# RWKV output products grouped with the heads in turn, tokens of block two's second half made early, and the adaptive vectors moved beside the first feed-forward half

## The chip, the cores and the metric

One core of a Trainium2 chip runs the whole program; the other cores are idle. The metric is the device time of one execution in microseconds (us). All values are 32-bit floats in memory. A large matrix product is done as three products of a split operand (high and low part, "fp32r"): `lo*high`, `high*lo`, `high*high`, all added up in PSUM. The small products (RWKV, attention, gated linear attention) are plain float32, and TensorE executes each of them as two passes, so 128 float32 products in the source are 256 matmul rows in the profile.

## The reference, cut to what matters

Two blocks follow each other on 1024 tokens of width 1024. Block one: RMS norm, one input projection, sliding-window attention with 8 heads (2 key heads), an RWKV-7 recurrence with 8 heads of 64, an output projection, and a convolution-gated feed-forward part of width 4096. Block two: an RMS norm that is scaled and shifted by "adaptive" vectors, an input projection, two gated linear attentions, a stick-breaking attention, an output projection and a final norm.

```python
# RWKV, per head and token (block one)
sa = einsum('bhvk,bhk->bhv', state, -kk_t)
state = state * w_t + sa[..., None] * (kk_t * a_t) + v_t[..., None] * k_t
o_t = einsum('bhvk,bhk->bhv', state, r_t)
# attention scores (block one)
scores = einsum('bnqhgd,bnkhd->bnhgqk', q, kb) * HEAD_DIM ** -0.5 + bias
# adaptive vectors and the tokens of block two
ada = silu(c) @ w_ada + b_ada                  # (1, 1024) @ (1024, 3072)
shift, scale, gate = split(ada, 3)
h = rms_norm_2(x) * (1.0 + scale) + shift
p = h @ w_in                                   # block two's projection
```

## The kernel before, in words

The program is recorded by generators ("streams") that `weave` steps in turn, each by a clock of its own: a `yield 5.2` moves the stream 5.2 units ahead, and the stream that stands earliest is stepped next. A scheduler then fixes the order on each engine from what was recorded, with priorities (`tc.high_priority(offset=...)` lets a part go ahead of what was recorded before it). Each engine runs its list in order. All loads and stores go through one queue, SyncE's (SP), also in order. Three stages follow each other.

**Stage one** (to about 592 us): the projection of block one (`proj1`, products `g`, L151), attention (`attention`, score products L664 into `a_ps`), RWKV for the first half of the tokens in three streams `rwkv_a`, `rwkv_b`, `rwkv_c`, and the output projection of the first half (`out_rows`).

**Stage two** (592 to about 1930 us): the feed-forward part, one half of the tokens after the other (`ffn`: products `g` with `w_up`, products `d` with `w_down`). Beside the first half runs RWKV for the second half of the tokens (`rest`). `between` waits until that is done, then makes the output projection of the second half, norms it for the second feed-forward half, computes the adaptive vectors (`ada_vectors`), and later begins block two's projection for the first half.

**Stage three** (from about 1930 us): block two. `fill` issues block two's remaining projection units of the first half (`units(0, ORD[0])`, 18 of them), then `proj2(1)`, which norms, scales, shifts and transposes the four 128-token tiles of the second half (`pre2`, `to_h`), then the units of the second half and the output projection. Beside it run the gated attentions (`gla_a`, `gla_b`, `gla_c`) and the stick-breaking attention (`stick`).

`rwkv_c` works on 128 tokens (a chunk pair, `e` = 0 to 7) in two steps `c` of 64 tokens. Heads lie in pairs: head `h` of a pair stands in partitions 64h to 64h+63, and the four pairs are counted by `j`. Per step there are four groups of eight products: with the state `St` for the solve (L594), the state update (`ra<-UV,BKt`, L601), and the output in two parts that add up in PSUM, `AR*St` (L606, contraction over one head's 64 rows) and `MT*UV` (L608, contraction over 128 rows). `ou[0]` and `ou[1]` are the PSUM tiles of the two heads. L606 and L608 alternate, product by product.

`ada_vectors` loads `w_ada` in 24 pieces of 512 KB (`wa`, two buffers), multiplies each with a column of `c` and adds it up on VectorE (`adam`, L81), sums over the partitions with a product by ones (L950), adds the bias and stores the vector.

Helper lines: L75 is every ScalarE activation, L78 tensor-tensor, L81 scalar-tensor-tensor and L85 tensor-scalar on VectorE, L125 the power on GpSimd, L135 the load of a weight piece (`wr`), which ScalarE and VectorE split into `wh` and `wl`; three such buffers are in use in turn.

## Time and profile before

| | |
|---|---|
| time, median of 3 runs | 2600.23 us (2585.8 to 2609.15) |
| the profiled execution | 2600.69 us |
| its span, first to last instruction | 2598.9 us |
| mean granted TensorE clock in it | 0.968 |
| TensorE (PE) busy | 2480.5 us, 95% |
| VectorE (DVE) busy | 1695.4 us, 65% |
| ScalarE (ACT) busy | 1171.0 us, 45% |

The profile shows this one execution. "PE" is the time in which a matmul is under way, "PEld" the loading of its stationary operand, which overlaps. A row `g<-hi,wl` reads: written `g`, read `hi` and `wl`. A line number is one of the kernel before. The granted clock is the share of TensorE's full clock that its throttle lets through. A row of the timeline gives the start in us, the time from the first start to the last end in us, engine, line, operation, tiles, shapes, the number of instructions in a row (x), and the idle time ahead of it with what ended it. In the order of a program, a row stands for one product (or xN for N equal ones in a row), and has no time.

### The profile page before, as it was taken

How to read it: one execution, taken by the hardware profiler on the slowest of the kernel's cores; microseconds unless marked ns; L12 is line 12 of the kernel's file. 1: busy time of each engine (PE TensorE's matmuls, PEld its weight loads, DVE VectorE, ACT ScalarE, POOL GpSimd, SP SyncE). 2: the span in 40 equal slices, each digit the busy share in tenths (PEclk: the TensorE clock that was granted, in tenths of full speed). 3: DMA queues.
4: the chain of work that ended last, by engine and by line, in shares of the span. 5: the costliest groups of instructions: out<-in, count | busy, mean ns of one | idle time of the engine just before them, and what ended most of it. 6: DMA issues, size and time to landing. Idle time of an engine off the chain costs nothing.

```text
span 2598.9 us, 40965 instructions
## 1 busy us (share of the span) xinstructions
PE 2480.5 (95%) x15310; PEld 1940.4 (75%) x15310; DVE 1695.4 (65%) x3676; ACT 1171.0 (45%) x2205; POOL 99.4 (4%) x138
## 2 busy tenths in 40 slices
PE   7999999899999999999988999999999989999987
PEld 5777777678787787878776888778887766777665
DVE  5466653664675674755687655545567897878887
ACT  4344332463433533334443333443345665566864
POOL 1001000000000000000000000000000000000000
PEclk9999998889999999999999999999999989999988
DMA  6433223542232332324486432243346425342437
GB/s 205 145 111 102 69 77 100 159 128 81 86 97 72 94 94 69 96 70 130 136 278 199 130 98 94 83 130 121 94 139 208 132 97 159 123 129 77 143 132 251
DMA packets 219998, 320.78 MB, mean 123 GB/s; under 512 B 56956, under 2 KB 95508, under 8 KB 219799
## 3 DMA queue, kind: packets, MB, share of 16 engines
q1 hardware_dynamic: 219798, 318.17, 38.9%
q8 instruction: 120, 1.97, 0.3%
q14 instruction: 80, 0.65, 0.1%
HBM read 270.88 MB, written 47.21 MB: 122 GB/s over the span
## 4 chain that ended last, share of the span: by engine, by line
PE 73%; DVE 10%; issue 6%; DMA 4%; ACT 4%; POOL 2%; SPq 0%; POOLq 0%; DVEq 0%; ACTq 0%
PE g L151 37%; PE d L151 11%; PE gr L743 2%; DVE wl L78 1%; PE gr L744 1%; PE gr L745 1%; DMA wa<-in_w_ada_dram 1%; PE ou L608 1%; PE ou L606 1%; PE R L1463 1%; PE ra L495 1%; PE s L1359 1%; PE a_ps L698 1%; DMA wr<-in_w_out_dram 1%; PE x L743 1%
## 5 line engine op out<-in xcount | busy, mean ns | idle before, releaser
L75 ACT ACTIVATE wh<-wr 128x512 fp32r<-128x512 f32 x712 | 443.7, 626 | 664.3 <-PE g L151 223.2
L151 PE MATMUL g<-hi,wl 128*128 128x512 f32 (+1 forms) x1680 | 678.0, 404 | 7.9 <-DVE wl L78 3.4
L151 PE MATMUL g<-hi,wh 128*128 128x512 f32 (+1 forms) x1680 | 668.9, 398 | 0.0
L151 PE MATMUL g<-lo,wh 128*128 128x512 f32 (+1 forms) x1680 | 667.6, 397 | 0.0
L78 DVE TENSOR_TENSOR wl<-wr,wh 128x512 fp32r<-128x512 f32 x712 | 484.4, 684 | 224.9 <-ACT wh L75 223.1
L151 PEld LDWEIGHTS g<-hi,wl 128*128 128x128 f32 (+1 forms) x1680 | 317.6, 189 | 86.3 <-issue 6.3
L151 PEld LDWEIGHTS g<-hi,wh 128*128 128x128 f32 (+1 forms) x1680 | 317.5, 189 | 72.5 <-issue 3.1
L151 PEld LDWEIGHTS g<-lo,wh 128*128 128x128 f32 (+1 forms) x1680 | 317.8, 189 | 71.6 <-issue 5.1
L81 DVE SCALAR_TENSOR_TENSOR cv<-g,CW,cv 128x511 f32<-128x511 f32 (+1 forms) x256 | 190.5, 744 | 186.0 <-ACT cv L75 185.8
L151 PE MATMUL d<-hh,wl 128*128 128x512 f32 x512 | 204.1, 403 | 7.1 <-DVE wl L78 2.2
L151 PE MATMUL d<-hl,wh 128*128 128x512 f32 x512 | 202.8, 396 | 0.1
L151 PE MATMUL d<-hh,wh 128*128 128x512 f32 x512 | 201.9, 395 | 0.0
L75 ACT ACTIVATE cv<-g,CW 128x512 f32<-128x512 f32 x128 | 99.5, 777 | 195.3 <-PE g L151 195.1
L78 DVE TENSOR_TENSOR acc<-d,acc 128x512 f32<-128x512 f32 x112 | 76.5, 688 | 83.4 <-PE d L151 83.3
L151 PEld LDWEIGHTS d<-hh,wl 128*128 128x128 f32 x512 | 96.9, 190 | 34.3 <-DVE acc L78 4.4
L151 PEld LDWEIGHTS d<-hl,wh 128*128 128x128 f32 x512 | 97.2, 190 | 22.5 <-DVE hl L78 2.8
L151 PEld LDWEIGHTS d<-hh,wh 128*128 128x128 f32 x512 | 97.1, 190 | 20.2
L743 PE MATMUL gr<-wl,hi 128*128 128x512 f32 x200 | 84.7, 424 | 6.3 <-DVE wl L78 4.6
L744 PE MATMUL gr<-wh,lo 128*128 128x512 f32 x200 | 81.0, 405 | 1.7 <-DVE lo L78 1.7
L745 PE MATMUL gr<-wh,hi 128*128 128x512 f32 x200 | 80.4, 402 | 0.0
L125 POOL TENSOR_TENSOR rs<-ms,half_c 128x1 f32<-128x1 f32 x48 | 31.1, 650 | 1129.4 <-DVE ms L85 1118.7
L75 ACT ACTIVATE hh<-cv 128x512 fp32r<-128x512 f32 x64 | 40.4, 631 | 70.1 <-DVE cv L78 69.7
(484 smaller groups left out, 3634.0 us busy)
## 6 DMA issues: line engine op xcount, KB each, us to landing
wr<-in_w_up_dram SPq DMA_DIRECT2D x256, 256.0 KB, 2.7
wr<-in_w_in_dram SPq DMA_DIRECT2D x160, 256.0 KB, 2.8
wr<-in_w_down_dram SPq DMA_DIRECT2D x128, 256.0 KB, 2.7
wr<-in_w_out_dram SPq DMA_DIRECT2D x100, 256.0 KB, 2.9
wr<-in_w_values_dram SPq DMA_DIRECT2D x64, 256.0 KB, 2.8
xt<-x SPq DMA_DIRECT2D x24, 512.0 KB, 4.6
wa<-in_w_ada_dram SPq DMA_DIRECT2D x24, 512.0 KB, 4.7
xt<-in_x_dram SPq DMA_DIRECT2D x16, 512.0 KB, 3.7
```

What stands on the lines that cost most here:

```text
L75: S.activation(out=out, in_=in_, func=func, **kw)
L78: (eng or V).tensor_tensor(out=out, in0=in0, in1=in1, op=op)
L81: V.scalar_tensor_tensor(out=out, in0=in0, scalar=scalar, in1=in1, op0=op0, op1=op1)
L125: G.tensor_tensor(out=dst, in0=src, in1=half_c[0:src.shape[0], 0:src.shape[1]], op=ALU.pow)
L151: T.matmul(out=ps, lhsT=l, rhs=r, start=(first and n == 0), stop=(last and n == 3 * len(wk) - 1))
L495: T.matmul(out=gp[:, q, :], lhsT=flat(BK[hb:hb + 64, 4 * b + q, :, :]), rhs=flat(AR[hb:hb + 64, 4 * b + q, 0:2, :]), start=True, stop=True)
L606: T.matmul(out=ou[h][ob:ob + 64, 0, j, :], lhsT=AR[hb:hb + 64, 2 * j + c, 0, :], rhs=St[hb:hb + 64, j, :], start=True, stop=False)
L608: T.matmul(out=ou[h][ob:ob + 64, 0, j, :], lhsT=MT[:, 2 * j + c, h, 0:64], rhs=UV[:, 2 * j + c, hb:hb + 64], start=False, stop=True)
L698: T.matmul(out=pv[:, h, :], lhsT=pt[:, i, kb, :], rhs=vtok[:, n - 1 + kb, 64 * g:64 * g + 64], start=(kb == kbs[0]), stop=(kb == 1))
L743: T.matmul(out=p, lhsT=hi[:, k, tok], rhs=wl, start=first, stop=False)
L744: T.matmul(out=p, lhsT=lo[:, k, tok], rhs=wh, start=False, stop=False)
L745: T.matmul(out=p, lhsT=hi[:, k, tok], rhs=wh, start=False, stop=last)
```

## The change

- In `rwkv_c`, the products with the state (L594) go with the heads in turn instead of one head after the other; the eight products `AR*St` of the output (L606) are issued together, ahead of the state update, and the eight products `MT*UV` (L608) together behind it. Only the first product into each PSUM tile and step has the start flag.
- In `attention`, the score products of the two key heads, which lie in partitions 0 to 63 and 64 to 127, go in turn: two PSUM tiles are taken together, and four products fill them by turns.
- `ada_vectors` runs at the start of `between`, so beside the first feed-forward half and the RWKV of the second half, with 14 units of its clock behind each load; its sum over partitions uses `psd`, the PSUM tiles of `w_down`'s products.
- `proj2(1)` is split: `prepare2` norms, scales and shifts the four tiles of block two's second half behind the eleventh unit of `units(0, ...)`, two of them in `xs` buffers and two in place in `xt` buffers; `proj2(1)` then only transposes them, at a priority of 250 ahead. `rstd_halves` is code that stood in `pre1` and is now called from both places.

Lines of the changed kernel are numbered a little higher: L594, L601, L606, L608 and L664 became L601, L616, L610, L621 and L676; L135, L151, L78, L81 and L85 became L137, L153, L80, L83 and L87.

```diff
+NP2, AP2 = 11, 250
+YA = 14
...
         for c in range(2):
             ob = 64 * c
+            for j in range(4):
+                for h in range(2):
+                    hb = 64 * h
+                    T.matmul(out=ou[h][0:64, 1, j, :], lhsT=AR[hb:hb + 64, 2 * j + c, 1, :], rhs=St[hb:hb + 64, j, :],
+                             start=True, stop=True)
             for h in range(2):
                 hb = 64 * h
-                for j in range(4):
-                    T.matmul(out=ou[h][0:64, 1, j, :], lhsT=AR[hb:hb + 64, 2 * j + c, 1, :], rhs=St[hb:hb + 64, j, :],
-                             start=True, stop=True)
                 tt(UV[0:64, c:8:2, hb:hb + 64], ou[h][0:64, 1], UV[0:64, c:8:2, hb:hb + 64], ADD)
+
+            for j in range(4):
+                for h in range(2):
+                    hb = 64 * h
+                    T.matmul(out=ou[h][ob:ob + 64, 0, j, :], lhsT=AR[hb:hb + 64, 2 * j + c, 0, :], rhs=St[hb:hb + 64, j, :],
+                             start=j == 0, stop=True, skip_group_check=True)
             sp = psr_t([128, 4, 64])
...
             for j in range(4):
                 for h in range(2):
                     hb = 64 * h
-                    T.matmul(out=ou[h][ob:ob + 64, 0, j, :], lhsT=AR[hb:hb + 64, 2 * j + c, 0, :], rhs=St[hb:hb + 64, j, :],
-                             start=True, stop=False)
                     T.matmul(out=ou[h][ob:ob + 64, 0, j, :], lhsT=MT[:, 2 * j + c, h, 0:64], rhs=UV[:, 2 * j + c, hb:hb + 64],
-                             start=False, stop=True)
+                             start=False, stop=True, skip_group_check=True)
...
-            for w in range(4):
-                g = w % 2
-                sp = psa_t([128, 2, 256])
...
+            for w in (0, 2):
+                sps = [psa_t([128, 2, 256]) for _ in range(2)]
                 for i in range(2):
...
+                    for g in range(2):
+                        T.matmul(out=sps[g][:, i, ko:], lhsT=qt[64 * g:64 * g + 64, w + i, :],
+                                 rhs=kT[64 * g:64 * g + 64, k0:k0 + nk], start=True, stop=True)
...
+        def total(w, m):
+            bb = ap.tile([128, D], F32, name="wa", bufs=2)
+            SY.dma_start(out=bb, in_=a["b_ada"][:, w * D:(w + 1) * D].broadcast_to([128, D]))
+            yield YA
+            for b in range(2):
+                ps = psd_t([128, 512])
...
-                yield 1.5
...
+                yield YA
+            yield from total(w, m)
...
     def between():
 
         nonlocal ap, shp, ps_x, evp
+        pa = ExitStack()
+        ap = pool("ap", 1, stack=pa)
+        yield from ada_vectors()
+        pa.close()
         yield from after(("c", 7))
...
         py.close()
-        pa = ExitStack()
-        ap = pool("ap", 1, stack=pa)
-        yield from ada_vectors()
-        pa.close()
+        yield 0.1
         yield from after(("g", 1, G1))
...
+    def prepare2():
+
+        yield from need1_x2()
+        scale1, shift = pre2_weights()
+        for i in range(4):
+            if i < 2:
+                xs = new_xs()
+                pre2(4 + i, xs, scale1, shift)
+            else:
+                xs = xt_load(x2_d[4 + i])
+                r = rstd_halves(xs)
+                stt(xs, xs, r, scale1, MUL, MUL)
+                tt(xs, xs, shift, ADD)
+            ready.append(xs)
+            yield 1.5
...
             hi, lo = new_h()
-            w = pre2_weights()
             for i in range(4):
-                xs = new_xs()
-                pre2(4 + i, xs, *w)
-                to_h(xs, i, hi, lo)
-                yield 3
+                with tc.high_priority(offset=AP2):
+                    to_h(ready.pop(0), i, hi, lo)
+                yield 1
...
     def fill():
-        yield from units(0, ORD[0], psg_t)
+        yield from units(0, ORD[0][:NP2], psg_t)
+        yield from prepare2()
+        yield from units(0, ORD[0][NP2:], psg_t)
         yield from proj2(1)
```

Three places show how the instructions move. The first is TensorE in stage one, the output products of the first 128 tokens (`ou_1858` and `ou_1859` are the two heads' PSUM tiles; `ra` is the state update, `g` the projection). Before:

```order
L601 MATMUL ra<-UV,BKt 64x64 x7
L606 MATMUL ou_1859<-St,AR 64x64
L608 MATMUL ou_1859<-UV,MT 64x64
L608 MATMUL ou_1858<-UV,MT 64x64
L606 MATMUL ou_1859<-St,AR 64x64
L608 MATMUL ou_1859<-UV,MT 64x64
L606 MATMUL ou_1858<-St,AR 64x64
L608 MATMUL ou_1858<-UV,MT 64x64
L606 MATMUL ou_1859<-St,AR 64x64
L608 MATMUL ou_1859<-UV,MT 64x64
```

The same place in the changed program (`ou_1864` and `ou_1865` are the two heads), and behind it the second step:

```order
L610 MATMUL ou_1864<-St,AR 64x64 x4
L610 MATMUL ou_1865<-St,AR 64x64 x4
L616 MATMUL ra<-UV,BKt 64x64 x8
L621 MATMUL ou_1864<-UV,MT 64x64
L621 MATMUL ou_1865<-UV,MT 64x64
L621 MATMUL ou_1864<-UV,MT 64x64
L621 MATMUL ou_1865<-UV,MT 64x64
```

```order
L610 MATMUL ou_1864<-St,AR 64x64 x4
L621 MATMUL ou_1864<-UV,MT 64x64 x4
L700 MATMUL a_ps<-C,st 128x128 x2
L610 MATMUL ou_1865<-St,AR 64x64 x4
L621 MATMUL ou_1865<-UV,MT 64x64 x4
```

The alternation of two kinds of product is gone: a kind now comes in runs of four or eight. Of the 128 products of L610 over all 16 steps, 88 stand in 22 runs of four, 32 in 4 runs of eight, and 8 in runs of one and seven; of those of L621, 72 stand in 18 runs of four, 48 in 6 runs of eight, and 8 in runs of three and five. The products of L610 go one head after the other, not in turn; those of L601, with the state, go in turn everywhere.

The second place is the queue of SyncE at the start of the first feed-forward half (`CW` are the convolution's weights, `wr` a piece of `w_up` or `w_down`, `mixk` and `xt` rows of activations, `wa` a piece of `w_ada`). Before:

```order
L845 DMA CW<-in_params_dram 128x256
L737 DMA mixk<-mix_d_133 128x512 x2
L135 DMA wr<-in_w_up_dram 128x512 x10
L135 DMA wr<-in_w_down_dram 128x512 x6
L463 DMA AR<-rkv_d_2_131 128x2x64 x3
```

In the changed program:

```order
L859 DMA CW<-in_params_dram 128x256
L968 DMA wa<-in_w_ada_dram 128x1024 x2
L236 DMA xt<-in_x_dram 128x1024
L137 DMA wr<-in_w_up_dram 128x512
L968 DMA wa<-in_w_ada_dram 128x1024 x2
L137 DMA wr<-in_w_up_dram 128x512
L968 DMA wa<-in_w_ada_dram 128x1024
L137 DMA wr<-in_w_up_dram 128x512
L968 DMA wa<-in_w_ada_dram 128x1024
L137 DMA wr<-in_w_up_dram 128x512 x2
L968 DMA wa<-in_w_ada_dram 128x1024 x2
L137 DMA wr<-in_w_up_dram 128x512 x2
```

The eight loads of the first vector stand one for one among the first `w_up` pieces of the half. The loads of the second and the third vector stand further behind, each again by turns with one `wr` piece.

The third place is VectorE in stage three, where the tokens of block two's second half are made (`xs` or `xt` is a tile of 128 tokens, `rs` its norm factor, `gbc` the scale, `shift` the shift; `PT`, `se`, `mk`, `XL` belong to the attentions). Before, the first two tiles are made early, and the last two stand among the stick-breaking attention's work, right ahead of their transposes:

```order
L81 SCALAR_TENSOR_TENSOR xs<-xt,rs,gbc 128x1024
L1367 TENSOR_REDUCE PT<-mk 128x64
L78 TENSOR_TENSOR xs<-xs,shift 128x1024
L81 SCALAR_TENSOR_TENSOR se<-w,se 128x2x128
L85 TENSOR_SCALAR ms<-ss 128x1
L1395 TENSOR_REDUCE ssn<-tmp 128x8
L78 TENSOR_TENSOR se<-se,C_16659 128x2x128
L81 SCALAR_TENSOR_TENSOR xs<-xt,rs,gbc 128x1024
```

In the changed program the last two tiles stand right behind the first two, some 260 rows earlier:

```order
L80 TENSOR_TENSOR xt<-xt,shift 128x1024
L80 TENSOR_TENSOR wl<-wr,wh 128x512
L80 TENSOR_TENSOR ms<-ss_17752 128x1
L80 TENSOR_TENSOR wl<-wr,wh 128x512
L87 TENSOR_SCALAR ms<-ms 128x1
L83 SCALAR_TENSOR_TENSOR xt<-xt,rs,gbc 128x1024
L80 TENSOR_TENSOR xt<-xt,shift 128x1024
```

On TensorE the stretch without any projection product `g` ahead of `proj2(1)` goes from 219 products to 131, counted product by product.

More of the change, by code (lines that the diff above doesn't have):

```diff
@@ L313, in pre1 @@
                 xs = xt
[L314 to L322 removed]
+                r = rstd_halves(xt)
             stt(xs, xt, r, gbc, MUL, MUL)
```

59 lines of the change are left out of this document (30 added, 29 removed).

## The prediction

> **What bounds the kernel now.** I read the busy times first, then the chain of work that ended last, then windows that cut the span into stages.
>
> ```profile
> PE 2480.5 (95%) x15310; PEld 1940.4 (75%) x15310; DVE 1695.4 (65%) x3676; ACT 1171.0 (45%) x2205; POOL 99.4 (4%) x138
> PE 73%; DVE 10%; issue 6%; DMA 4%; ACT 4%; POOL 2%; SPq 0%; POOLq 0%; DVEq 0%; ACTq 0%
> ```
>
> TensorE (PE) is busy 95% of the span and holds 73% of the chain, so time taken off TensorE counts, where it lies on the chain. The windows show how that differs by stage. Columns are the stretch and its length, then busy us and instruction count of PE, weight load, VectorE, ScalarE and GpSimd, the granted TensorE clock, the DMA engines' share and GB/s.
>
> ```profile
> 40.00:592.00 552.00, 526.60 (x3402) 412.00 (x3400) 317.60 (x910) 232.70 (x524) 38.26 (x56) 0.93 0.38 116
> 592.00:1266.00 674.00, 669.06 (x3679) 533.82 (x3679) 402.23 (x836) 259.44 (x436) 20.11 (x23) 0.99 0.30 89
> 1300.00:1420.00 120.00, 104.76 (x430) 80.22 (x429) 94.89 (x144) 41.72 (x77) 4.29 (x7) 0.93 0.74 243
> 2112.00:2146.00 34.00, 29.11 (x363) 22.33 (x363) 31.94 (x60) 26.58 (x54) 2.80 (x3) 0.80 0.39 132
> ```
>
> Stage one (first row) has PE idle 25 of 552 us and a clock of 0.93. The first feed-forward half (second row) is bound by PE alone: 669 of 674 us busy at full clock. The third row is the stretch in which the adaptive vectors are computed: PE idles 15.2 us of 120, and the clock falls. The fourth lies ahead of block two's second half: PE idles 4.9 of 34 us, the clock is 0.80, and VectorE is 94% busy. These four are where the change acts.
>
> **The output products (L594, L606, L608).** The timeline shows what alternation costs:
>
> ```profile
> 222.41 0.32 PE L606 MATMUL ou<-St,AR 64*64 64x64 f32 x2
> 222.66 0.33 PE L608 MATMUL ou<-UV,MT 128*64 128x64 f32 x2
> ...
> 224.97 0.66 PE L507 MATMUL ra<-C,AR 128*128 128x128 f32 x4
> ...
> 222.03 0.45 PE L608 MATMUL ou<-UV,MT 128*64 128x64 f32 x4
> ...
> 225.67 0.96 PE L594 MATMUL ou<-St,AR 64*64 64x64 f32 x16
> 226.56 0.44 PE L511 MATMUL ra<-C,BK 128*128 128x128 f32 x2
> ...
> 232.28 0.69 PE L601 MATMUL ra<-UV,BKt 128*64 128x64 f32 x16
> 232.89 0.66 PE L698 MATMUL a_ps<-vtok,pt 128*128 128x64 f32 x4
> ```
>
> From 222.41 to 224.97 stand ten turns of one product (two passes) each: 0.256 us a turn. The one turn with two products (222.03, ended by 222.41) takes 0.38, so a further pass of the same kind costs 0.06 us; the switch is what is dear. A step `c` has 16 turns, 4.10 us; 16 steps make 65.6 us. In the new order a run of four products of one head is eight passes, 0.256 + 6 x 0.06 = 0.62 us. A run of eight of the kind L606, one head after the other, costs what L594 costs now, 225.67 to 226.56, 0.89 us. Eight of the kind L608 use all 128 rows whichever head it is, 0.256 + 14 x 0.06 = 1.10 us. With the runs counted in the order (40 of four, 4 and 6 of eight, four odd ones of about 0.6) the sum is 24.8 + 3.6 + 6.6 + 2.4 = 37.4 us. Saved: 28 us, 14 in each of stages one and two.
>
> L594 with the heads in turn: the row for that is L601, whose two heads also go to different halves of the array by turns, and which takes 0.61 us for 16 passes against 0.89. I take 0.28 x 16 = 4.5 us, 2.2 a stage. The halves differ (rows there, columns here), so the bounds are 0 and 0.45 us a step, half of the 0.89.
>
> A cost: VectorE's addition into `UV` for head 0 could start after eight passes and must now wait for sixteen, some 0.3 us later a step. L606 no longer needs `UV` and stands ahead of the state update on PE, so it covers that; without the cover it would be 16 x 0.3 = 5 us.
>
> How much of this is on the path? The chain of waits, cut to the two stages:
>
> ```profile
> by line: PE g L151 25.1%; issue 16.8%; PE a_ps L698 4.2%; PE a_ps L664 3.4%; DMA wr<-in_w_out_dram 2.8%; PE ra L495 2.6%; PE a_ps L686 2.4%; PE ou L606 2.3%; PE ou L608 2.2%; DMA xt<-in_x_dram 1.8%; POOL rn L125 1.6%; DVE wl L78 1.6%; POOL
> by line: PE g L151 47.1%; PE d L151 22.1%; PE ou L608 2.5%; PE ou L606 2.5%; PE x L744 2.1%; PE x L745 2.1%; PE x L743 2.1%; PE ra L495 1.9%; PE ou L594 1.1%; issue 1.1%; PE ra L601 0.9%; DVE ot L78 0.9%; DVE XT L78 0.9%; PE ra L429 0.8%; D
> ```
>
> In stage two (second row) L606 and L608 hold 5.0% of 674 us, 33.7, which is all of their 32.8. In stage one (first row) they hold 4.5% of 552, 24.8 us, three quarters. So stage two gains 14 + 2.2 = **16.2 us**, stage one 0.75 x 16.2 = 12.2.
>
> **The score products (L664).** Two rows show both cases:
>
> ```profile
> 191.74 1.14 PE L664 MATMUL a_ps<-kT,qt 64*128 64x256 f32 x8
> 192.81 0.50 PE L151 MATMUL g<-hi,wl 128*128 128x512 f32 x1
> ...
> 194.18 1.13 PE L664 MATMUL a_ps<-kT,qt 64*128 64x256 f32 x4 [0.18 <-DVE mx L668]
> 195.24 0.50 PE L151 MATMUL g<-lo,wh 128*128 128x512 f32 x1
> ```
>
> Eight passes of both heads by turns take 1.07 us, four passes of one head 1.06: by turns two heads run at once. There are 32 fours. In the order before, 14 of them already stand beside the other head; the other 18 would save up to half, 18 x 0.43 = 7.7 us (0.43 rather than 0.53, because a lone pair still pays its start and end). With L664's share of the chain, 3.4% of 552 = 18.8 us of some 27, that is **5 us**. VectorE takes two more score tiles at once from the same two PSUM buffers; nothing is added.
>
> [...]
>
> **The adaptive vectors.** First what they cost where they stand; the rows are from the products L151 alone, the groups of instructions, and the waits of that stretch:
>
> ```profile
> 1300.00:1420.00 120.00, 92.28 (x366) 70.89 (x365) 0.93 0.74 243
> 1420.00:1930.00 510.00, 481.09 (x2075) 385.18 (x2074) 1.00 0.34 107
> L81 DVE SCALAR_TENSOR_TENSOR adam<-wa,sc,adam 128x1024 f32<-128x1024 f32 x21 | 26.9, 1281 | 9.1 <-DMA wa<-in_w_ada_dram 8.9
> L950 PE MATMUL x<-adam,ones 128*128 128x512 f32 x12 | 8.1, 812 | 5.9 <-DVE adam L81 5.9
> SPq L939 <- DVE adam L81: 16.9, 13, 1.8
> ```
>
> The rest of that half does 2075 feed-forward products in 510 us, 4.07 a us; 366 products are 90 us of such work, and the transposes beside them 2. So the stretch loses 28 us, 8.1 of them the sums on PE themselves. Some belongs to the end of the first half, which runs there too (its norm and its stores), so I take 24, between 15.2 (the idle time alone) and 28.
>
> [...]
>
> In the first half the 8.1 us on PE come back in full, as PE is 99% busy there. The loads and the 24 VectorE operations lie beside it. Where do they collide?
>
> ```profile
> 600.00:626.00 26.00, 26.00 (x127) 21.39 (x126) 15.38 (x27) 13.44 (x21) 0.00 (x0) 1.00 0.31 91
> 776.00:830.00 54.00, 53.72 (x431) 41.80 (x430) 26.33 (x51) 18.64 (x30) 0.74 (x5) 1.00 0.22 65
> ```
>
> The first vector's rows fall beside the first row here. VectorE would have 15.4 + 7 x 1.28 + 0.75 = 25.1 us of work in 26, and the DMA engines 2.4 + 4.2 MB, 27 us at the 243 GB/s seen above. It just does not fit. SyncE's queue is in order, so a `wa` load that waits for VectorE to free its buffer holds the `w_up` pieces behind it, and PE waits for those. I put 4 us on it. The second vector falls about where the second row lies: 26.3 + 9.7 of 54 us on VectorE and 142 GB/s. It fits; 1 us each for it and the third. The sums take a buffer of `psd` six times, but the vector is then long ready. Together 8.1 + 6 = 14 us come back; a net gain of **10 us**, with bounds from -13 (every vector as dear as in the old place, 28) to +20 (only the 8.1 come back).
>
> **The tokens of the second half.**
>
> ```profile
> 2111.90 0.39 PE L151 MATMUL g<-hi,wh 128*128 128x512 f32 x1
> ...
> 2121.56 0.27 PE L232 MATMUL trx<-C,xs 128*128 128x128 f32 x1
> 2132.67 1.54 PE L232 MATMUL trx<-C,xs 128*128 128x128 f32 x6
> ...
> 2145.58 0.40 PE L151 MATMUL g<-hi,wl 128*16 128x512 f32 x1
> ```
>
> For 33.7 us PE has no projection product. Between the transposes of the first two tiles and of the last two lie 11.1 us, in which tiles three and four are made. In the order the products of the attentions in that stretch fall from 219 to 131; at the same pace it takes 20.2 us, 13.5 less. But those 88 products still have to be done elsewhere. What is surely lost now is 4.9 us of idle PE and a fifth of 29.1 us by the clock, 10.7 in all; and two tiles, 2 x (1.28 + 1.22) = 5.0 us, leave a VectorE that is 94% busy. I take **7 us**, between 0 and 13.5. Two more squares and two additions (the tiles in `xt` are squared in halves) cost under 1 us on engines that wait there.
>
> **The sum.** 12.2 + 5 + 16.2 + 10 + 7 = 50.4 us off the profiled execution's 2600.7 us (its span 2598.9 and 1.8 around it; the median is 2600.2): 2550 us. The bounds of the terms add up to 2527 and 2586 if all went one way except the adaptive vectors' lowest, which is a rival.
>
> **The rivals.**
>
> *Stage one gains nothing* (chance 0.17). PE is less busy there, 16.8% of its chain is "issue", and the state runs through VectorE; freed PE time would turn into waits for `UV`, `St` and the score tiles. Against it: PE is 95% busy, and L606, L608 and L664 stand on the chain. Then 16.2 + 10 + 7 = 33 us: 2568.
>
> *The clock comes back as well* (0.15). Stage one ran at 0.93 of the clock, 7% of 552 = 38 us. If packed products remove the low stretches, up to that much comes on top; with two thirds of it, 2525.
>
> *The loads of `w_ada` hold up the weights* (0.04, the slower side). Place: SyncE's queue in the first feed-forward half, where no idle PE time covers it. Each load there costs its wait for VectorE plus its flight; on the chain of the old stretch one such round is 4.3 to 5.1 us of flight and 1.3 of VectorE. If all 24 were exposed, 24 x 6 = 144 us come back instead of 6: 2688. It decides from 56 us on, 2.4 us a load; that all are exposed is unlikely, as SyncE's 13 waits for `adam` average 1.3 us now. With half of them exposed: about 2616.
>
> *Nothing comes of it* (0.02): new waits take the place of the old, 2600.
>
> **How the numbers follow.** The forecast, 2550, has 0.62, with 2527 to 2578 as its own spread. A measurement tells about 1% from no change, 26 us (the three runs shown span 23). Below 2574 lie most of the forecast (0.56), two thirds of the first rival (0.11) and the second (0.15): faster 0.82. The rest of these and the last are within 1%, 0.14; slower 0.04. The range reaches from 2515, into the second rival, to 2582, which takes in the first.
>
> **What would show it.** Right: L610 and L621 hold about 37 us instead of 66, in runs of x8 and x16; the first feed-forward half gets shorter by 2 us only, since 16 go and 14 come; the stretch ahead of 1420 loses its `wa` loads, and PE is over 97% busy there at full clock; the gap without projection products shrinks to some 20 us. Wrong: waits of SyncE for `adam` of several us, and PE below 97% at the start of the first half; PE idle time in stage one up by 10 us; or heads that do not overlap, the state products (L601 there) still at 0.89 us a step.

## The result, and the profile after

The changed kernel takes 2532.46 us (median of 4 runs, 2526.18 to 2538.22) where the kernel before, on the same chip, takes 2604.6. The ratio is **0.9734** [0.9691, 0.9776]. In six later runs, again beside the kernel before, it was 0.9736 [0.9697, 0.9775]. The profiled execution took 2526.18 us, its span is 2524.4: 74.5 us less than the profiled span before. The forecast was 2550, a gain of 50, with a range from 2515 to 2582.

The page's first and fourth part, the busy times and the chain's shares by engine:

```profile
PE 2416.4 (96%) x15310; PEld 1899.2 (75%) x15310; DVE 1689.7 (67%) x3678; ACT 1171.2 (46%) x2209; POOL 98.4 (4%) x138
PE 76%; DVE 9%; issue 5%; ACT 4%; DMA 3%; POOL 2%; SPq 0%; POOLq 0%; DVEq 0%; ACTq 0%
```

PE does the same 15310 products in 64 us less, and it is still the bound. To see where the time went, I cut both spans at the same three places in the program: the first product of a down projection (`d<-hh,wl`), the first transpose of `ffn_end` (`d<-C,acc`), and the last product of a down projection. The four rows are then stage one with what lies around it, the first feed-forward half, the second, and stage three. Windows of before, then of after (columns as in the prediction: length, busy us of PE, weight load, VectorE, ScalarE and GpSimd, granted clock, DMA share, GB/s):

```profile
0.00:649.30 649.30, 607.04 (x3792) 473.81 (x3793) 364.81 (x999) 270.00 (x587) 42.62 (x70) 0.94 0.39 118
649.30:1304.70 655.40, 648.88 (x3528) 517.51 (x3527) 407.05 (x841) 259.66 (x441) 25.90 (x31) 0.99 0.31 96
1304.70:1925.30 620.60, 600.67 (x2595) 480.41 (x2594) 380.57 (x618) 235.51 (x389) 5.86 (x10) 0.99 0.41 132
1925.30:2598.90 673.60, 623.86 (x5401) 468.63 (x5398) 542.93 (x1218) 405.84 (x788) 25.00 (x28) 0.96 0.46 148
```

```profile
0.00:624.70 624.70, 579.25 (x3792) 457.49 (x3793) 374.37 (x1007) 269.79 (x587) 41.87 (x71) 0.95 0.43 131
624.70:1266.20 641.50, 635.53 (x3539) 506.36 (x3538) 425.16 (x864) 260.11 (x441) 26.26 (x31) 1.00 0.37 112
1266.20:1863.80 597.60, 587.86 (x2583) 473.57 (x2582) 349.93 (x587) 235.12 (x389) 4.45 (x9) 1.00 0.36 113
1863.80:2524.40 660.60, 613.71 (x5400) 461.77 (x5398) 540.23 (x1220) 406.21 (x792) 25.78 (x28) 0.98 0.46 151
```

| stretch | before | after | difference | predicted |
|---|---|---|---|---|
| up to the first down projection | 649.3 | 624.7 | -24.6 | -17.2 |
| first feed-forward half | 655.4 | 641.5 | -13.9 | -2.2 (16.2 off, 14 back) |
| second feed-forward half | 620.6 | 597.6 | -23.0 | -24 |
| stage three | 673.6 | 660.6 | -13.0 | -7 |

Twelve products and 31 VectorE instructions have left the third row: these are the adaptive vectors. The products and 23 of the 31 are in the second row now, the eight of the first vector in the first (the trace lacks one matmul record). In all four rows the granted clock is higher than before, by 0.01 or 0.02.

**The output products after.** The timeline of PE where a step `c = 0` and a part of a step `c = 1` stand:

```profile
215.91 0.96 PE L610 MATMUL ou<-St,AR 64*64 64x64 f32 x16
216.81 0.69 PE L616 MATMUL ra<-UV,BKt 128*64 128x64 f32 x16
217.32 1.10 PE L621 MATMUL ou<-UV,MT 128*64 128x64 f32 x16
218.35 0.33 PE L514 MATMUL ra<-C,AR 128*128 128x128 f32 x1
218.61 0.68 PE L601 MATMUL ou<-St,AR 64*64 64x64 f32 x16
219.22 0.55 PE L514 MATMUL ra<-C,AR 128*128 128x128 f32 x3
...
219.98 0.68 PE L610 MATMUL ou<-St,AR 64*64 64x64 f32 x8
220.58 0.68 PE L621 MATMUL ou<-UV,MT 128*64 128x64 f32 x8
221.19 0.44 PE L700 MATMUL a_ps<-C,st 128*128 128x128 f32 x2
```

Read from start to start, L610 takes 0.90 us and L621 1.03 for sixteen passes, and 0.60 and 0.61 for eight. The prediction had 0.89, 1.10 and 0.62. L601, with the heads in turn, ends in 0.61 us, as taken. What it had not: the state update L616 now stands in one run with L621 behind it, which has its shapes (128 rows, 64 columns), and takes 0.51 us instead of 0.61.

**The groups of PE's instructions** that the change touched, after:

```profile
L676 PE MATMUL a_ps<-kT,qt 64*128 64x256 f32 x112 | 28.8, 434 | 6.3 <-DVE mx L682 6.3
L621 PE MATMUL ou<-UV,MT 128*64 128x64 f32 x256 | 20.6, 230 | 0.0
L610 PE MATMUL ou<-St,AR 64*64 64x64 f32 x256 | 19.9, 230 | 0.1
L616 PE MATMUL ra<-UV,BKt 128*64 128x64 f32 x256 | 13.5, 230 | 0.0
L601 PE MATMUL ou<-St,AR 64*64 64x64 f32 x256 | 13.1, 235 | 0.0
L957 PE MATMUL d<-adam,ones 128*128 128x512 f32 x12 | 6.3, 610 | 0.0
```

The products of `ou` hold 53.6 us now. The score products (first row) are as long as before, and PE waits 6.3 us ahead of them; the row of before:

```profile
L664 PE MATMUL a_ps<-kT,qt 64*128 64x256 f32 x112 | 28.7, 424 | 0.6 <-DVE mx L668 0.6
```

I also summed the time from each PE instruction's start to the next one's, cut at 0.45 us: L606 and L608 took 68.0 us before, L610 and L621 36.7 after; L594 15.4, L601 11.2; the state update 14.1 and 9.1; the scores 28.3 and 28.2.

**The clock.** Each timed run comes with the clock that TensorE was granted on the mean of its span. Between runs of one and the same kernel it varies, and the time with it. Over the 141 timed runs of the experiments below (12 kernels, and the kernel before beside each of three groups of them), within each kernel, a run with 0.01 more clock is 19.7 us shorter (standard error 0.6); that line accounts for 91% of the variance within a kernel, and leaves 2.7 us. With it a difference can be split into what goes with the clock and what is left at an equal clock. It is a statistical split, not an experiment: the clock may itself follow from what a kernel does, and then the split takes a part of the kernel's own gain away. The changed kernel's six later runs have a mean clock of 0.9767, the kernel before beside them 0.9664. Of the 67.2 us between their means, 20.3 go with the clock; **46.9 us** are left.

### The profile page after: what moved, and what is told of

Same layout as the page of the kernel before. It is cut to its first block, busy times and chain, and to the rows that moved or that the text cites. A ratio compares the mean times of both kernels' runs of the same rounds, so it can differ in the third digit from the quotient of the medians.

```text
span 2524.4 us, 40941 instructions
## 1 busy us (share of the span) xinstructions
PE 2416.4 (96%) x15310; PEld 1899.2 (75%) x15310; DVE 1689.7 (67%) x3678; ACT 1171.2 (46%) x2209; POOL 98.4 (4%) x138
## 4 chain that ended last, share of the span: by engine, by line
PE 76%; DVE 9%; issue 5%; ACT 4%; DMA 3%; POOL 2%; SPq 0%; POOLq 0%; DVEq 0%; ACTq 0%
PE g L153 39%; PE d L153 12%; PE gr L757 2%; PE gr L758 2%; PE gr L759 2%; DVE wl L80 1%; PE ra L502 1%; PE R L1504 1%; PE s L1400 1%; PE a_ps L712 1%; PE a_ps L676 1%; PE x L757 1%; PE x L759 1%; PE x L758 1%; PE z L1489 1%
## 5 line engine op out<-in xcount | busy, mean ns | idle before, releaser
L153 PE MATMUL g<-hi,wl 128*128 128x512 f32 (+1 forms) x1680 | 674.9, 402 | 7.2 <-ACT ev L77 2.4
L153 PE MATMUL g<-hi,wh 128*128 128x512 f32 (+1 forms) x1680 | 667.1, 397 | 0.0
L153 PE MATMUL g<-lo,wh 128*128 128x512 f32 (+1 forms) x1680 | 665.4, 396 | 0.0
L80 DVE TENSOR_TENSOR wl<-wr,wh 128x512 fp32r<-128x512 f32 x712 | 484.4, 685 | 209.2 <-ACT wh L77 207.3
L153 PEld LDWEIGHTS g<-hi,wl 128*128 128x128 f32 (+1 forms) x1680 | 316.0, 188 | 83.4 <-ACT ev L77 5.5
L153 PEld LDWEIGHTS g<-hi,wh 128*128 128x128 f32 (+1 forms) x1680 | 316.0, 188 | 71.5 <-issue 2.9
L153 PEld LDWEIGHTS g<-lo,wh 128*128 128x128 f32 (+1 forms) x1680 | 316.3, 188 | 70.5 <-issue 4.6
L83 DVE SCALAR_TENSOR_TENSOR cv<-g,CW,cv 128x511 f32<-128x511 f32 (+1 forms) x256 | 190.6, 745 | 189.0 <-ACT cv L77 188.9
L153 PE MATMUL d<-hh,wl 128*128 128x512 f32 x512 | 202.0, 398 | 4.5 <-DVE acc L80 1.6
L153 PE MATMUL d<-hl,wh 128*128 128x512 f32 x512 | 201.2, 393 | 0.3 <-DVE hl L80 0.2
L153 PE MATMUL d<-hh,wh 128*128 128x512 f32 x512 | 200.5, 392 | 0.0
L80 DVE TENSOR_TENSOR acc<-d,acc 128x512 f32<-128x512 f32 x112 | 76.5, 688 | 78.4 <-PE d L153 78.4
L153 PEld LDWEIGHTS d<-hh,wl 128*128 128x128 f32 x512 | 95.5, 188 | 31.8 <-ACT hh L77 5.2
L153 PEld LDWEIGHTS d<-hl,wh 128*128 128x128 f32 x512 | 96.2, 188 | 22.6 <-DVE hl L80 3.6
L153 PEld LDWEIGHTS d<-hh,wh 128*128 128x128 f32 x512 | 96.2, 188 | 19.8
```

The lines of the kernel that those rows point to most:

```text
L80: (eng or V).tensor_tensor(out=out, in0=in0, in1=in1, op=op)
L83: V.scalar_tensor_tensor(out=out, in0=in0, scalar=scalar, in1=in1, op0=op0, op1=op1)
L153: T.matmul(out=ps, lhsT=l, rhs=r, start=(first and n == 0), stop=(last and n == 3 * len(wk) - 1))
```

## The experiments

Each kernel was timed in six runs, three of the parts alone in twelve, beside 11 or 29 runs of the kernel before. "At equal clock" is the difference of the means less 1975 us times the difference of the clocks; from the 2.7 us of spread and the slope's error it is known to about 3 us.

| kernel | ratio to before | clock (before) | difference of means | at equal clock |
|---|---|---|---|---|
| the change again | 0.9736 [0.9697, 0.9775] | 0.9767 (0.9664) | -67.2 | -46.9 |
| output products undone | 0.9844 [0.9809, 0.9879] | 0.9770 (0.9645) | -37.9 | -13.4 |
| score products undone | 0.9747 [0.9713, 0.9780] | 0.9740 (0.9645) | -64.8 | -46.1 |
| adaptive vectors undone | 0.9741 [0.9707, 0.9775] | 0.9773 (0.9645) | -66.3 | -41.1 |
| tokens undone | 0.9757 [0.9725, 0.9789] | 0.9728 (0.9645) | -62.1 | -45.7 |
| output products alone | 0.9825 [0.9780, 0.9870] | 0.9720 (0.9667) | -44.6 | -34.2 |
| score products alone | 0.9979 [0.9951, 1.0006] | 0.9689 (0.9667) | -6.3 | -1.9 |
| adaptive vectors alone | 0.9967 [0.9932, 1.0002] | 0.9671 (0.9667) | -10.1 | -9.4 |
| tokens alone | 0.9942 [0.9909, 0.9975] | 0.9720 (0.9667) | -13.9 | -3.4 |
| both heads in one tile | 0.9673 [0.9636, 0.9711] | 0.9822 (0.9664) | -85.2 | -54.0 |
| the same, scores pinned | 0.9725 [0.9686, 0.9765] | 0.9780 (0.9664) | -71.7 | -48.7 |
| adaptive vectors, dense | 0.9856 [0.9815, 0.9897] | 0.9708 (0.9664) | -37.6 | -28.8 |

### The change again

No edit.

> The changed kernel once more, on the chip and beside the kernel before, so that the parts undone can be set against it. Theory A (the parts add up: the products 40, the scores 3 to 5, the adaptive vectors 14, the tokens 13, as the stages of the traces show): about 0.972 of before, 2538 where before takes 2612. Rival B (the four undone parts measured so far give back only 30, 1, 1 and 6 against 0.9734, so the profiled execution of the change was a lucky one): 0.976 or more. Rival C (the parts help each other through the clock): below 0.970.

0.9736: rival B's "0.976 or more" lies within the interval, C's "below 0.970" hardly. The four parts undone give back, in ratio, 1.1, 0.1, 0.1 and 0.2%, together 1.5% of 2.6. At equal clock they give back 33.5, 0.8, 5.8 and 1.2, together 41.3 of 46.9. The parts done alone bring 34.2, 1.9, 9.4 and 3.4, together 48.9. So **the parts add up**, once the clock is set apart; in raw times the undone parts give back 37.7 of 67.2 us and the parts alone bring 74.9. The profiled execution of this run took 10 us longer in stage three than the one of the first (670.7 against 660.6, at a clock of 0.97 against 0.98) with nothing changed.

### The output products, undone and alone

```diff
-            for j in range(4):
-                for h in range(2):
-                    T.matmul(out=ou[h][0:64, 1, j, :], ... rhs=St[hb:hb + 64, j, :], ...)
             for h in range(2):
+                for j in range(4):
+                    T.matmul(out=ou[h][0:64, 1, j, :], ... rhs=St[hb:hb + 64, j, :], ...)
...
-            for j in range(4):
-                for h in range(2):
-                    T.matmul(out=ou[h][ob:ob + 64, 0, j, :], lhsT=AR[...], rhs=St[...], start=j == 0, ...)
...
+                    T.matmul(out=ou[h][ob:ob + 64, 0, j, :], lhsT=AR[...], rhs=St[...], start=True, stop=False)
                     T.matmul(out=ou[h][ob:ob + 64, 0, j, :], lhsT=MT[...], rhs=UV[...], start=False, ...)
```

> The changed kernel with the products of the RWKV output and state as before (alternating kinds, one head after the other); all else as changed. Theory of freed TensorE time: in the profile after, these products and the state update take about 40 us less from start to start than before (L606 and L608 68.0 to 36.7, L594 15.4 to 11.2, the state update 14.1 to 9.1), nearly all on the path: 35 to 40 us slower than the changed kernel, about 2568 to 2572. The prediction's terms: 12.2 + 16.2 = 28 us slower, 2561. Rival, that the freed time only becomes waits in stage one: 16 to 20 us, about 2550, and all of it in the first feed-forward half.

> The kernel before with the output products' new order alone. Undoing this part took 1.1% of the time back, the stages of that trace lost 21 us in stage one and 24 in the first feed-forward half. Theory A (the parts add up; 35 us of PE from L594, L606 and L608, 5 from the state update, and some of the clock): 40 us, a ratio of 0.984 or 0.985, half of it before the first feed-forward product and half in the first feed-forward half. Rival B (only the sum predicted, 28 a ratio of 0.989, without state update and clock). Rival C (it needs the other parts to bring the clock back): 0.99 or more.

Undone, 1.1% comes back, 29 us in raw time, nearer to the prediction's 28 than to the 35 to 40 of the theory; alone, it brings 1.75%. At equal clock both say **34 us**. The rival's 16 to 20 us are out. The windows of the kernel with this part alone, stage one and the first half:

```profile
0.00:636.00 636.00, 587.40 (x3793) 463.79 (x3794) 364.42 (x999) 269.68 (x587) 41.34 (x70) 0.93 0.41 120
636.00:1270.50 634.50, 628.07 (x3527) 503.03 (x3526) 406.38 (x841) 259.76 (x441) 26.28 (x31) 1.00 0.34 99
```

The first half is 20.9 us shorter than before, and PE's busy time falls by as much: all of it was on the path there. In stage one PE is busy 19.6 us less, but the stretch is only 13.3 shorter: 6.3 us turned into waits. That is the three quarters' argument of the prediction, measured: 13.3 of 19.6 is two thirds. Theory A of "alone" (40, half and half) was near in the raw time (45), though the two stretches share it as 13 and 21, and its 5 us for the state update show in the same way: its group holds 13.5 us here too, 16.3 before.

### The score products, undone and alone

```diff
-            for w in (0, 2):
-                sps = [psa_t([128, 2, 256]) for _ in range(2)]
+            for w in range(4):
+                g = w % 2
+                sp = psa_t([128, 2, 256])
                 for i in range(2):
-                    for g in range(2):
-                        T.matmul(out=sps[g][:, i, ko:], ...)
+                    T.matmul(out=sp[:, i, ko:], ...)
...
```

> The changed kernel with the attention's score products as before, one key head's tile after the other. Theory: the scheduler put the two products of a head together again in 10 of the 16 pairs, and the score products take 28.2 us from start to start in both profiles; no difference beyond 3 us, about 2532. The prediction's term: 5 us slower, 2537. Rival, that taking two score tiles at once holds up the other users of the two PSUM buffers: up to 5 us faster.

> The kernel before with the score products' new order alone. Theory A (the scheduler puts a head's products together again, as in the changed kernel): within 0.2% of before, 0.998 to 1.002, PE time of the score products unchanged at 28 us. Rival B (the 5 us predicted): 0.998, PE time 21 us. Rival C (VectorE gets four score tiles' work in one piece and the state's sums wait behind it): slower, 1.002 or more, PE idle time in stage one up.

Undone 0.1%, alone 0.2% with an interval that holds 1; 0.8 and 1.9 us at equal clock. PE's time for these products did change, against both expectations. Their group with the part undone, then with the part alone:

```profile
L677 PE MATMUL a_ps<-kT,qt 64*128 64x256 f32 x112 | 31.2, 438 | 1.4 <-DVE mx L681 1.4
L663 PE MATMUL a_ps<-kT,qt 64*128 64x256 f32 x112 | 25.7, 425 | 0.2 <-DVE mx L669 0.2
```

The new order takes 2.4 us off PE in the changed kernel (31.2 to 28.8) and 3.0 alone (28.7 to 25.7). That before and after agree (28.7 and 28.8) is a coincidence: with the output products' new order alone, the scores in their old order hold 31.3. In the changed kernel the idle time ahead of them takes more than that back: 6.3 us, and 1.4 with the part undone. The timeline of the changed kernel shows why the gain is so small. A piece by turns, and one in which each head's products stand together again:

```profile
244.63 0.70 PE L676 MATMUL a_ps<-kT,qt 64*128 64x256 f32 x4
245.26 0.91 PE L553 MATMUL rb__2362<-XQ,MT 32*32 32x32 f32 x23
```

```profile
505.26 1.88 PE L676 MATMUL a_ps<-kT,qt 64*128 64x256 f32 x8
507.07 0.49 PE L758 MATMUL gr<-wh,ml 128*128 128x512 f32 x1
```

By turns four passes take 0.63 us; the eight of the other piece take 1.81, and in the trace only the two passes at the change of head start together, at 506.01 us. In the changed order only 6 of the 16 pairs of tiles stand by turns. In the other 10 the scheduler took both products of the first head and then both of the second; that it did so because the second PSUM tile comes free later is likely, but was not shown.

### The adaptive vectors, undone and alone

```diff
     def between():
-        pa = ExitStack()
-        ap = pool("ap", 1, stack=pa)
-        yield from ada_vectors()
-        pa.close()
...
         py.close()
+        pa = ExitStack()
+        ap = pool("ap", 1, stack=pa)
+        yield from ada_vectors()
+        pa.close()
```

The undone kernel also has the 1.5 after each load and the sums in `ps_x` of before.

> The changed kernel with the adaptive vectors at their old place and spacing, beside the second feed-forward half. Theory that their loads and additions hide wholly in the first half: the second half takes back the 23 us it lost, the first half gives back 3 to 5 (the sums on TensorE): 18 to 22 us slower, about 2550 to 2554, with the granted clock falling in that stretch again. The prediction's term: 10 us slower, 2542, with 14 us given back in the first half. Rival, that the second half was faster for other reasons (its clock): under 5 us.

> The kernel before with the adaptive vectors moved alone. Undoing this part cost the timed runs only 0.05%, although the trace's second half lost 20 us and the first half gained 6. Theory A (net 13 us, as the two halves' lengths say, and the timed difference of the undoing is its uncertainty): 0.995, second half near 600 us, first half near 662. Rival B (what is gained comes back through the clock elsewhere): second half near 600 us, yet a ratio of 0.998 to 1.000. Rival C (the net 10 predicted): 0.996, first half longer by 14.

The two feed-forward halves with this part alone:

```profile
671.30:1328.80 657.50, 650.81 (x3539) 516.15 (x3538) 425.42 (x864) 259.84 (x441) 25.86 (x31) 1.00 0.36 110
1328.80:1928.10 599.30, 589.31 (x2583) 474.72 (x2582) 349.99 (x587) 235.16 (x389) 4.43 (x9) 1.00 0.36 112
```

The second half gives 21.3 us, the first takes 2.1 back. Undone, the same: the second half is 617.6 us long, 20.0 more than with the change, the first 635.3, 6.2 less. In all fourteen profiles the second half takes 598 to 603 us with the vectors moved (nine) and 617 to 621 without (five). With the output products' new order the first half takes 635 us without the vectors and 641 to 643 with them (the kernels of the last section apart, and the next one, where the vectors lie ahead of that half). By the halves the net is 14 to 19 us; the timed runs say less, 0.9 (undone) and 10.1 (alone), at equal clock 5.8 and 9.4. So the 18 to 22 us expected of the undoing did not come. For the part alone the interval rules out none of the three ratios, but the first half got longer by 2 us, not by 14. A part of the difference is the clock: in the second half before it is granted 0.99, 1% of 620 us, and the line above sets such time apart.

### The adaptive vectors at the new place, but dense

```diff
     def total(w, m):
...
-            yield YA
...
-            yield YA
+            yield 1.5
         for w in range(3):
...
-                yield YA
+                yield 1.5
```

> The adaptive vectors at their new place, but with the spacing of the old one (1.5 after each load in place of 14), so that all three fall into the first 100 us or so of the first feed-forward half. Theory A (what I feared: VectorE and the DMA engines just don't have the room there, and wa loads waiting in SyncE's queue hold up the w_up pieces): each vector costs some 4 us, 10 to 12 us more than the changed kernel, with PE idle at 630 to 730. Rival B (the queue and the engines have room enough, as in the changed kernel, where the give-back beyond the sums was about zero): within 2 us, first half 642 us as before.

0.9856: some 30 us slower than the change, 18 of them at equal clock. It is **theory A's side, but not its place**. The first feed-forward half is 640.2 us long, no longer than in the change. That says nothing of the room in it, because the sums now all run from 582 to 671 us, ahead of the first down projection. What is longer is the tail of stage one: the first down projection comes at 671.1 us where the change, in the run beside it, has it at 631.3. Windows of that tail, then PE's longest waits in it, then VectorE's timeline at one place:

```profile
600.00:620.00 20.00, 18.97 (x91) 14.23 (x89) 17.06 (x28) 7.48 (x13) 0.00 (x0) 1.00 0.72 220
640.00:660.00 20.00, 9.45 (x85) 7.75 (x83) 13.96 (x23) 3.19 (x5) 0.00 (x0) 0.74 0.64 184
```

```profile
PE ra L646 <- DVE og L80: 11.3, 1, 11.3
PE ou L610 <- DVE UV L80: 6.7, 3, 3.1
```

```profile
657.34 1.28 DVE L83 SCALAR_TENSOR_TENSOR adam<-wa,sc,adam 128x1024 f32<-128x1024 f32 x1 [0.51 <-DMA wa<-in_w_ada_dram]
658.54 0.42 DVE L80 TENSOR_TENSOR og<-ou,mu 128x256 f32<-128x256 f32 x1
```

In VectorE's list the sums of the adaptive vectors stand ahead of `Sn` (the new state), `og` (the output of the last tile) and the additions to `UV`. They take 34 us of VectorE's time there, against 9.7 in the change, and wait for their own loads: 7.0 us in nine waits for `wa`. PE's longest waits are for the `og` and the `UV` behind them. PE is busy 9.45 us of 20, and the clock is 0.74. With 14 after each load the 24 loads spread from 569 to 906 us, and in all of it VectorE waits 3.5 us for them, in four waits. So the spacing is what makes the new place cheap. PE's waits point to VectorE's list: for a weight piece PE waits 0.4 us. That SyncE's queue has no part in it is not shown, for from 600 to 680 us it waits 10.5 us in eight waits for `adam` ahead of `wa` loads, and the weight pieces go through the same queue.

### The tokens, undone and alone

```diff
         else:
             hi, lo = new_h()
+            w = pre2_weights()
             for i in range(4):
-                with tc.high_priority(offset=AP2):
-                    to_h(ready.pop(0), i, hi, lo)
-                yield 1
+                xs = new_xs()
+                pre2(4 + i, xs, *w)
+                to_h(xs, i, hi, lo)
+                yield 3
...
-        yield from units(0, ORD[0][:NP2], psg_t)
-        yield from prepare2()
-        yield from units(0, ORD[0][NP2:], psg_t)
+        yield from units(0, ORD[0], psg_t)
```

> The changed kernel with the tokens of block two's second half made where they were before. Theory that the gap without projection products, with its waits and its half clock, is lost time: 12 to 14 us slower (stage three took 673.6 us from the last product of w_down before, 660.6 after), about 2545. The prediction's term: 7 us slower, 2539. Rival, that stage three is bound by VectorE, which does the same work in both: under 3 us.

> The kernel before with the tokens of the second half made early alone. Undoing this part took 0.2% back. Theory A (the gap without projection products gets shorter by the two tiles, 7 us as predicted): 0.997. Rival B (the whole gap's 13 us, as the trace of stage three says): 0.995. Rival C (work that another stage has to do instead): 0.999 or more.

The gap without projection products is shorter than predicted, 15.0 us instead of 20.2 (33.7 before). From the timeline of the change, and the window of that gap:

```profile
2051.25 0.40 PE L153 MATMUL g<-hi,wh 128*128 128x512 f32 x1
...
2066.28 0.40 PE L153 MATMUL g<-hi,wl 128*16 128x512 f32 x1 [0.97 <-DVE lo L80]
```

```profile
2051.00:2066.50 15.50, 14.19 (x225) 10.94 (x224) 12.48 (x24) 11.20 (x23) 0.00 (x0) 1.00 0.30 100
```

The clock there is 1.00, it was 0.80. Alone, the part takes stage three from 673.6 to 660.9 us, undone it is 674.1: 13 us against the first profile of the change, as theory B had it, but only 3 against its repeat (670.7). All fourteen profiles together say more:

| stage three in the profiles | profiles | length, us | granted clock |
|---|---|---|---|
| tokens made early | 9 | 660.4 to 670.7, mean 663.7 | 0.97 to 0.99 |
| tokens as before | 5 | 673.4 to 677.2, mean 674.9 | 0.95 to 0.96 |

The two groups do not overlap, in length or in clock, whatever else was changed. So here **the higher clock goes with the part**. It is 11 us on the mean, and 0.02 of the clock on 660 us is about as much. The timed runs bring 13.9 us alone and 5.1 undone; at equal clock 3.4 and 1.2 are left, but this split takes away what the part gains through the clock. What left the gap is done elsewhere, as the prediction feared; what the change brings here is mostly clock.

### Both heads in one tile, and the scores pinned

```diff
-        ou = [psc.tile([128, 2, 4, 64], F32, name=f"ou{h}") for h in range(2)]
+        ou2 = psc.tile([128, 2, 2, 4, 64], F32, name="ou")
+        ou = [ou2[:, h] for h in range(2)]
```

> Both heads' products go to one tile of two PSUM banks, so that all runs stand with the heads in turn: in the changed kernel half of the steps (c = 1) still have four runs of four products, 0.60 us each, 2.4 us a step. Theory A (a switch between the two kinds costs 0.2 us, and heads by turns overlap if they use different rows): a step with c = 1 takes 0.6 + 1.05, a saving of 0.75; L610 in steps with c = 0 goes from 0.9 to 0.6; 8 x 0.75 + 8 x 0.3 = 8.4 us, 7 us on the path: 0.9972 of the changed kernel. Rival B (the order within a run does not matter, heads do not overlap): L610 stays at 0.9 in x16, only the c = 1 steps gain, 8 x 0.45 = 3.6. Rival C (one tile makes VectorE's sum for head 0 wait for head 1): no gain, waits for UV up by 0.3 us a step.

```profile
218.36 0.68 PE L611 MATMUL ou<-St,AR 64*64 64x64 f32 x16
218.97 0.62 PE L617 MATMUL ra<-UV,BKt 128*64 128x64 f32 x13
```

Theory A holds in size: L611 (L610 in the change) takes 0.61 us for sixteen passes, with the heads in turn, where it took 0.90 with one head after the other. Its sixteen products of each kind now stand in whole runs in both values of `c`. Summed from start to start, the three groups (`AR*St`, `MT*UV` and the state update) take 38.6 us instead of 45.7. At equal clock the kernel is **7.1 us** faster than the change, 7 were expected; the timed runs, with a clock of 0.982, say 0.9673 against 0.9736. None of the state's products waits for VectorE's `UV`, so rival C is out. This is the fastest of all the kernels.

The second kernel adds a pin, so that the scores stand by turns in all 16 pairs:

```diff
-                        T.matmul(out=sps[g][:, i, ko:], ...)
+                        mm = T.matmul(out=sps[g][:, i, ko:], ...)
+                        if i or g:
+                            tc.keep_in_program_order(mm)
```

> As heads_one_tile, and the score products are pinned behind one another in the order of the program, so that the two heads really alternate in 16 of 16 pairs, not in 6. Theory A (the scores gained nothing because the scheduler put the products of a head together again): 10 pairs go from 1.81 to 1.26 us, 5.5 us of PE, about 4 on the path beyond heads_one_tile. Rival B (PE now waits in order for the second PSUM buffer, which VectorE frees later): waits of 0.5 us or more ahead of the products, no gain or a loss of up to 5 us. Rival C (the emptying of PSUM is the bound): the products shorter, the stage as long as before.

The score products get shorter, as theory A says. Their group in the first kernel, then in the second:

```profile
L677 PE MATMUL a_ps<-kT,qt 64*128 64x256 f32 x112 | 28.3, 435 | 4.7 <-DVE mx L683 4.7
```

```profile
L677 PE MATMUL a_ps<-kT,qt 64*128 64x256 f32 x112 | 25.6, 426 | 1.1 <-DVE mx L685 0.9
```

PE does them in 2.7 us less and waits 3.6 less ahead of them, and yet the kernel is slower: 5.3 us at equal clock, 0.9725 against 0.9673. The windows of both up to the first down projection:

```profile
0.00:622.90 622.90, 575.79 (x3792) 453.98 (x3793) 374.02 (x1007) 270.20 (x587) 41.88 (x71) 0.95 0.45 131
```

```profile
0.00:624.30 624.30, 574.27 (x3793) 449.66 (x3794) 374.06 (x1007) 269.82 (x587) 43.04 (x71) 0.95 0.44 131
```

PE's busy time falls by 1.5 us, its idle time rises by 2.9, from 47.1 to 50.0. Part of it can be named: the products of `ra` waited 0.3 us for VectorE's `MT` in the one and 4.1 in the other. The stretch is 1.4 us longer. Of the two profiled spans the pinned kernel's is 3.0 us longer: stage three, where nothing was edited, takes 3.9 us more and the two feed-forward halves 2.3 less. So theory A's 4 us on the path did not come; rivals B and C both fit that, they were not told apart, and where the rest of the 5 us goes is not shown.

## Why the prediction was right, point by point

The time came out 18 us below the forecast and within the range. The work was judged about right; the clock was counted only where a term held some of it.

- **The output products: right, a little too small.** 28.4 us were forecast on the path (14 + 2.2 in the first half, 12.2 in stage one); 34 were measured, undone as well as alone. L606 and L608 went from 68.0 to 36.7 us (65.6 to 37.4 forecast), L594 saved 4.2 (4.5). The step that was missing is the state update, 5.0 us, which now stands beside products of its own shapes. The price of a switch, 0.256 us against 0.06 for a further pass, carried the term.
- **Stage one's three quarters: right.** Two thirds of PE's saving there came through. The first rival (stage one gains nothing) is out.
- **The score products: the step failed.** "The other 18 would save up to half" supposed that the new order in the program is the order on PE. It was so in 6 pairs of 16: 2.4 to 3.0 us of PE's time came where 7.7 were forecast, and in the changed kernel the waits ahead of them are 6.3 us, where they are 1.4 with the part undone. 1 or 2 us came instead of 5. Those 6.3 us PE waits for VectorE's `mx`. Even where the order was forced, no time came of it.
- **The adaptive vectors: the net was right, both sides were not.** The second half gave 20 to 23 us (24 forecast), the first took back 2 to 7, not 14. Of the 14, 8.1 was the busy time of the sums, from a row whose 12 products overlap and whose last four ran at a clock of 0.50 (1.06 us and more each, against 0.59): in the new place they hold 6.3 us, and 4.3 from start to start. The 6 for collisions were about zero with the loads 14 apart. At equal clock the net is 6 to 9, forecast 10; that it comes so near is in part luck, since the gain and what comes back were both put too high. The first half got shorter by 13.9 us and not by 2, because the output products gave 20.9 there instead of 16.2 and about 7 came back instead of 14.
- **The third rival** (loads hold up the weights) did not happen in the change, and something like it does in the dense kernel, but with another place and a smaller price: 30 us more than the change where the rival had 66 and more, and by PE's waits the sums on VectorE held up the last tile of stage one; what the loads in SyncE's queue added was not told apart.
- **The tokens: right in kind, and about right in size.** The gap shrank to 15.0 us (20.2 forecast). 7 us were forecast; 13.9 came alone and 5.1 undone, and stage three is 11 us shorter in the profiles with the part. The 1 to 3 us at equal clock do not measure this term, because more than half of what it starts from, 5.8 of 10.7 us, was the low clock of the gap, and that is what came.
- **The clock: the term that was mis-sized.** The sum counted it only inside the terms. It went up by 0.0103 on the mean of the runs, and 20.3 us go with that; the second rival had 25. The size agrees, the place does not: the rival meant stage one, where the clock is 0.94 before and 0.95 and 0.94 in the two profiles of the change, at most some 7 us of 650. The largest share lies in stage three, with the tokens. Beyond that, which part of the change brings the clock stays open. Done alone, the products and the tokens raise it by 0.0053 each, the scores by 0.0022, the vectors by 0.0004, but with six to twelve runs each the means are uncertain by about 0.003, and undoing any one of them lowers it by no more than that.
- **What would show it.** No sign of being wrong appeared: SyncE waited 5.9 us for `adam` in six waits, the longest 1.4; PE was without a gap from 624.7 to 660 us; its idle time in stage one rose by 3 us, not 10. One sign of being right failed, beside the first half's 2 us: PE's share ahead of the second half. The stretch that held the adaptive vectors runs at full clock now, but PE is at 96%, not over 97%:

```profile
1266.20:1386.20 120.00, 114.95 (x518) 92.22 (x517) 86.31 (x147) 54.41 (x97) 4.45 (x9) 1.00 0.48 159
```

## What to carry to other kernels

On a TensorE that is 95% busy, count the switches between product shapes, not only the products: a turn of two passes took 0.256 us where a further pass of the same kind took 0.06, and grouping them was worth more than everything else here together (34 of 46.9 us at equal clock). The order written in the program is not the order on the engine; read what the scheduler made of it before a gain is put on it, and where products must alternate, try one tile for both: for the output products it kept the order, where two tiles did not, and was worth 7.1 us. When differences are compared at equal clock, look also in which stage the clock rose: it can be the change's own gain. When moving background work beside a full engine, space it, so that no in-order queue holds a wait for its data ahead of the main work: with the loads 14 apart VectorE waited 3.5 us for them, with 1.5 it was 7.0, and 11.3 us of PE's time went in one wait for an `og` that stood behind the sums.

## What the runs showed of the hardware that was not expected

The clock is at half where PE is not idle. In the changed kernel, ahead of such a stretch and in it, then the same stretch in its repeat:

```profile
240.00:245.00 5.00, 4.43 (x26) 3.27 (x24) 4.16 (x8) 1.44 (x3) 1.59 (x6) 1.00 0.56 142
248.10:282.20 34.10, 34.10 (x210) 27.55 (x207) 10.63 (x28) 4.44 (x11) 0.00 (x0) 0.50 0.19 52
254.40:288.50 34.10, 34.10 (x205) 27.52 (x203) 10.50 (x28) 4.47 (x12) 0.00 (x0) 0.50 0.18 51
```

PE is busy throughout, and the clock stays at 0.50 for 34 us. In the 20 us ahead of it the longest wait was 1.47 us in the changed kernel's first profile. What it is that brings the low clock on, and what ends it, no run here tells. Some low stretches come at the same place in both profiles, like this one; others come in one alone: the repeat is at 0.50 from 2019 to 2029 us, while the first is at 1.00 all the way from 680 to 2370. In windows of 10 us, up to 2520 us in the first and 2540 us in the repeat, what the two profiles lack of the full clock adds up to 43.5 and 64.2 us; the windows below 0.8 hold 28.0 and 43.2 of it, so 15.2 of the 20.7 us between the two. Over the timed runs a run's mean clock goes with 91% of the variance within a kernel, at 19.7 us for 0.01; in which stretches the runs without a profile lose it is not shown.

The second is how far two heads overlap: products of 64 rows, one head in partitions 0 to 63 and the other in 64 to 127, take 0.61 us for sixteen passes by turns (L601 here, L611 with both heads in one tile), and 0.90 one head after the other (L610 here).
